# Scaling softmax rows in place on GpSimd, joining the scalars of two head pairs, and reweaving the matmul order of a hybrid attention layer

## The chip, the cores and the metric

The kernel runs on one NeuronCore of a Trainium2 chip. The metric is device microseconds (us) of one execution, from the first to the last instruction of the program. The engines have separate instruction queues: PE (TensorE, matmuls and transposes), DVE (VectorE), ACT (ScalarE), POOL (GpSimd) and SP (SyncE, which here only issues DMAs).

## The reference

One decoder layer on 512 tokens of width 1024, in float32: eight heads of block-sparse attention beside eight heads of a chunked Gated DeltaNet, both from one input projection, then an output projection, an RMS norm, and a squared-ReLU MLP between two further norms. Cut to what the change touches:

```python
h = rms_norm(x, w_first)
q, k, v, gdn_qkv, z, a, b = split(h @ w_in)

# attention: 512 tokens, 8 heads of 64; with a top-3 of 256-wide blocks all blocks are seen
s   = q @ k.T / 8 + rel_bias[distance]       # causal
att = softmax(s) @ v

# DeltaNet: a causal convolution of width 4 and silu on its q, k, v
q, k, v = silu(conv(gdn_qkv));  q, k = l2_normalize(q), l2_normalize(k)
beta, g = sigmoid(b), -exp(a_log) * softplus(a + dt_bias)   # per token and head
# chunks of 64 tokens: T = inverse of (1 + lower triangle of beta * k k^T * decay),
# then 8 chunks one after the other, with the state S (64x64 per head) carried along
o = rms_norm(gdn(q, k, v, beta, g)) * silu(z)

x1  = x + rms_norm(concat(att, o) @ w_out, post_mix)
u   = rms_norm(x1, pre_mlp)
out = x1 + rms_norm(relu(u @ w_up)**2 @ w_down, post_mlp)
```

## The kernel before

**Arithmetic.** Large operands are kept as a sum of two reduced-precision parts, `hi` and `lo`. `split(hi, lo, src)` (L112) copies `src` into `hi` on ACT and writes `lo = src - hi` with one DVE subtraction. A product of two such operands is three matmuls (`mm3`, L144). For weights that come from memory in pieces of 128x512 (`w_raw`), the `lo` part is made on DVE or on POOL; `LO_DVE` (L29) says for which numbers of pieces it is DVE.

**Tiles.** The 512 tokens lie along the columns, so one projection item is one bank of PSUM (128 output columns x 512 tokens, 24 matmuls of 512 columns). `ORDER` (L28) lists the items: `q`, `k`, `v`, `z` are DeltaNet's, `x`, `y` are attention's q and k, `w` is attention's v; the number is the pair of heads, since 128 rows are two heads of 64. `bank(tag)` gives out the eight banks of PSUM: two `mm` (projections), three `g` (DeltaNet), three `a` (attention).

**What sets the order.** PE's order is written out by hand. Every piece of the work is a Python generator (`projections`, `scores`, `values`, `chunks`, `inverse`, `scan`, `output`, ...), and `Weave.run` (L58) takes the next step of one after the other by the text `STEPS` (L20), passing over a generator whose `yield name` waits for a mark that isn't set yet. The matmuls run in exactly that order. The instructions of DVE, ACT, POOL and SP are put in order by a scheduler; `LEAD` gives the steps of a kind of generator a head start in its priorities. So a step that is put elsewhere in `STEPS` takes with it the matmuls, and the work of the other engines follows.

**Places that the change touches:**

- `scores` (L647) computes, for each pair `p`, four score blocks: row block q (128 tokens) against 128, 256, 384 or 512 keys, in the groups (3), (2) and (1, 0). A DVE instruction adds the bias and takes the minimum (`mins`, L675), ACT exponentiates in place in SBUF and adds up the rows (L677). After the last group DVE takes the reciprocals of the sums, ACT spreads them over 64 columns each (`R8`, L683).
- `values` (L688) turns the exponentials with PE transposes (L701; key block k of row blocks k to 3, so 2, 4, 6 and 8 transposes), ACT copies them to SBUF (`ph`, L704). Then four PE transposes turn `R8` (L720), ACT copies the result (L722), the products with V run into the bank `po` (L710), and DVE multiplies by the turned reciprocals (L728) before the split.
- `conv_silu` (L359) scales a projection's bank by the rms factor in place in PSUM, then ACT and three DVE instructions (L365) form the convolution from it. The bank is free after the last of them.
- `chunks` and `turned` (L551, L513), once per pair: ACT gathers the per-token scalars of one pair into `R`, four PE transposes turn it, ACT and DVE make `RC`, matmuls with the selecting matrix `sel` spread its rows (`rows`, L533), and `within` (L539) forms the products inside the 64-token chunks, from which come `NT` and `AT`. After pairs 1 and 3 `NT` goes to memory (`d_n`).
- `inverse` (L735) loads it back in another layout and inverts 32x32 triangles with 62 DVE instructions (`pr`, `inv`, L747 and L748), then stores the result (`d_u`, `d_t`). `scan` (L757) clears `UT` on POOL, loads the two results back, and combines them in two rounds of 32x32 matmuls (`ps_g<-uap,NT`, then `ps_g<-inv,uap`). POOL then makes `kB` and the decayed keys `kdec` for two pairs at a time (L806, L807), on which the matmuls `ps_g<-inv,kB` wait; then come the eight chunk steps.
- `normed` (L990), once per block t of 128 tokens after the output projection: square sums on ACT, the factor by two small POOL instructions (`rstd_of`, L170, with a power), the scaled sum with x on DVE, then the same again for the MLP's norm, and PE transposes.
- `up0` (L1039): the first 512 columns of the MLP's first product, in halves of 256 tokens, so that two blocks of tokens are enough to begin.

Of the kernel before, what the change touches and what calls it, by code (L numbers as in the profile page):

```python
# [21 lines left out]
LEAD = {'chunks': 25, 'inverse': 0, 'scan': 50, 'scores': 400, 'values': 300, 'finish_o': 400, 'take': 50, 'take_a': 300, 'scalars': 0}
TURNS = 0, 2, 1, 3, 4, 6, 5, 7
FILL = 7
SQUARES = {1: (0,), 2: (1,), 3: (2, 3), 4: (4, 5), 5: (6, 7)}
AT_SUM, AT_RSTD = (6, 0), (7, 1)
FIRST_BANKS = "mm g g a"
ORDER = "k0 q0 x0 y0 k1 q2 q1 k2 k3 z0 q3 x1 w0 v3 v0 v1 v2 y1 y2 x2 x3 y3 z2 z3 z1"  # L28
LO_DVE = (23, 51)  # L29
# [1506 lines left out]
```

## Time and profile before

| | |
|---|---|
| median of 3 runs | 612.99 us (612.47 to 614.84) |
| the profiled execution | 613.28 us |
| its span, first to last instruction | 611.5 us |
| granted TensorE clock | 0.999 |
| PE busy | 600.7 us (98%) |
| DVE, ACT, POOL busy | 481.2, 364.8, 140.9 us |
| bytes over DMA | 113.21 MB |

The stages by PE's rows: the head until some 28 us; the projections with the DeltaNet scalars, the scores and the chunk products until 166; the scan's two rounds and its chunk steps until 235, among the last projections; the output projection from 241 to 290; the first MLP group until some 311; the rest of the MLP until 605; then the last norm and the stores. A matmul's busy time includes its pipeline, so that two neighbours overlap: 512 columns show as 0.39 us busy, one beginning every 0.23 us. PE's share of 98% therefore counts overlapped and filled time, and its idle time is what tells.

### The profile page before, as it was taken

Reading aid. Unit: us, or ns where it says so; the run is one execution under the profiler, and the core shown is the slowest. Engines: PE = TensorE matmul, PEld = TensorE weight load, DVE = VectorE, ACT = ScalarE, POOL = GpSimd, SP = SyncE. Lnnn points to the kernel's source line nnn. Section 1 sums busy time; section 2 is a strip of 40 time slices with the busy share of each in tenths; the row PEclk is TensorE's granted clock in tenths of the full one; section 3 lists DMA queues with packets and bytes.
Section 4 is the critical chain, followed back from the end, with each engine's and each line's share of the span. In section 5 each row is a group of like instructions: output and inputs, shape, how many; then the busy total and the mean of one; then the engine's idle time right before and its main releaser. Section 6 shows DMA issues by size and latency. Waiting matters only on the chain.

```text
span 611.5 us, 11058 instructions
## 1 busy us (share of the span) xinstructions
PE 600.7 (98%) x4281; PEld 515.0 (84%) x4281; DVE 481.2 (79%) x692; ACT 364.8 (60%) x645; POOL 140.9 (23%) x180
## 2 busy tenths in 40 slices
PE   9999999999999999999999999999999999999995
PEld 7778788877778786888999999999998888888884
DVE  6688975999664866668799888787798888887776
ACT  7379772353677567444368565755575657565663
POOL 1557745001221111025022231122221310000000
PEclk9999999999999999999999999999999999999999
DMA  9332334227412124815879899998999999767503
GB/s 316 89 115 86 88 87 117 91 70 184 125 45 66 35 89 128 286 53 173 329 176 311 219 274 223 273 283 205 235 337 357 285 293 286 254 229 297 164 0 138
DMA packets 61156, 113.21 MB, mean 185 GB/s; under 512 B 15784, under 2 KB 35368, under 8 KB 60720
## 3 DMA queue, kind: packets, MB, share of 16 engines
q1 hardware_dynamic: 43120, 82.89, 40.0%
q0 software_dynamic: 17696, 29.36, 23.2%
q8 instruction: 33, 0.54, 0.4%
q10 hardware_dynamic: 288, 0.26, 0.1%
q14 instruction: 19, 0.16, 0.1%
HBM read 106.71 MB, written 35.15 MB: 232 GB/s over the span
## 4 chain that ended last, share of the span: by engine, by line
PE 58%; issue 9%; DMA 2%; ACT 2%; DVE 0%; POOLq 0%; SPq 0%
PE ps_mm L82 27%; PE ps_g L82 17%; PE ps_a L82 13%; DMA xy<-d_x 1%; DMA wo_raw<-in_w_out 1%; PE ps_a L85 1%; ACT wo_h L125 0%; ACT ph L704 0%; ACT L L677 0%; DVE wo_l L126 0%; DVE wdl L114 0%; ACT wdh L113 0%; PE ps_g L85 0%; POOLq L1532 0%; ACT ot L876 0%
## 5 line engine op out<-in xcount | busy, mean ns | idle before, releaser
L113 ACT CAST wdh<-wd 128x1024 fp32r<-128x1024 f32 x53 | 55.9, 1054 | 51.4 <-PE ps_mm L82 22.6
L113 ACT CAST u_h<-w 128x1024 fp32r<-128x1024 f32 x49 | 50.9, 1044 | 52.1 <-DVE w L1146 15.6
L114 DVE TENSOR_TENSOR wdl<-wd,wdh 128x1024 fp32r<-128x1024 f32 x53 | 64.9, 1224 | 21.6 <-ACT wdh L113 21.4
L114 DVE TENSOR_TENSOR u_l<-w,u_h 128x1024 fp32r<-128x1024 f32 x49 | 59.8, 1224 | 23.8 <-ACT u_h L113 23.8
L82 PE MATMUL ps_mm<-hT_h,w_hi 128*128 128x512 f32 x168 | 71.3, 424 | 1.3 <-DVE conv L365 1.0
L82 PE MATMUL ps_mm<-hT_h,w_lo 128*128 128x512 f32 x168 | 66.1, 394 | 0.0
L1179 POOL DMA_DIRECT2D d_T<-in_w_down x32 | 33.0, 1032 | 142.3 <-DMA d_T<-in_w_down 81.3
L82 PE MATMUL ps_mm<-hT_l,w_hi 128*128 128x512 f32 x168 | 65.7, 391 | 0.0
L137 ACT CAST w_hi<-w_raw 128x512 fp32r<-128x512 f32 x50 | 31.0, 620 | 46.1 <-DMA w_raw<-in_w_in 12.0
L82 PE MATMUL ps_mm<-wdh,u_h 128*128 128x512 f32 x116 | 45.3, 390 | 0.0
L82 PE MATMUL ps_mm<-wdl,u_h 128*128 128x512 f32 x116 | 45.1, 389 | 0.0
L82 PE MATMUL ps_mm<-wdh,u_l 128*128 128x512 f32 x116 | 45.1, 389 | 0.0
L82 PEld LDWEIGHTS ps_mm<-hT_h,w_hi 128*128 128x128 f32 x168 | 31.7, 189 | 12.4 <-issue 5.9
L82 PEld LDWEIGHTS ps_mm<-hT_h,w_lo 128*128 128x128 f32 x168 | 31.5, 188 | 7.5 <-DVE w_lo L138 0.4
L82 PEld LDWEIGHTS ps_mm<-hT_l,w_hi 128*128 128x128 f32 x168 | 31.8, 189 | 4.9
L138 POOL TENSOR_TENSOR w_lo<-w_raw,w_hi 128x512 fp32r<-128x512 f32 x23 | 29.7, 1291 | 20.3 <-ACT w_hi L137 17.4
L114 DVE TENSOR_TENSOR u_l<-f,u_h 128x1024 fp32r<-128x1024 f32 x28 | 34.1, 1218 | 0.0
L82 PE MATMUL ps_g<-wdh,u_h 128*128 128x512 f32 x80 | 31.1, 389 | 0.0
L82 PE MATMUL ps_g<-wdl,u_h 128*128 128x512 f32 x80 | 31.1, 389 | 0.0
L82 PE MATMUL ps_g<-wdh,u_l 128*128 128x512 f32 x80 | 31.1, 389 | 0.0
L113 ACT CAST u_h<-f 128x1024 fp32r<-128x1024 f32 x28 | 29.3, 1046 | 0.0
L138 DVE TENSOR_TENSOR w_lo<-w_raw,w_hi 128x512 fp32r<-128x512 f32 x27 | 21.4, 794 | 7.9 <-ACT w_hi L137 7.8
(486 smaller groups left out, 1830.2 us busy)
## 6 DMA issues: line engine op xcount, KB each, us to landing
d_T<-in_w_down POOLq DMA_DIRECT2D x48, 512.0 KB, 11.0
wd<-d_T SPq DMA_DIRECT2D x32, 512.0 KB, 6.2
w<-in_w_up SPq DMA_DIRECT2D x28, 512.0 KB, 7.6
wd<-in_w_down SPq DMA_DIRECT2D x24, 512.0 KB, 7.3
w_raw<-in_w_in SPq DMA_DIRECT2D x40, 256.0 KB, 2.6
wo_raw<-in_w_out SPq DMA_DIRECT2D x16, 256.0 KB, 3.5
d_T<-d_T POOLq DMA_DIRECT2D x8, 512.0 KB, 12.1
ww<-in_w_first SPq DMA_DIRECT2D x8, 256.0 KB, 5.3
```

Of the source, the lines that this page charges most:

```text
L82: nc.tensor.matmul(o, l, r, **kw)
L85: nc.tensor.transpose(o, i, ident[:k, :k])
L113: nc.scalar.copy(hi, src)
L114: tt(lo, src, f32(hi), op=OP.subtract)
L137: nc.scalar.copy(hi, raw)
L138: (sub or tt)(lo, raw, f32(hi), op=OP.subtract)
L1179: nc.gpsimd.dma_start(d_T[t][k], block(b, second)[k], accum_op=OP.add, max_dma_last_dim=1024)
```

## The change

- **Softmax.** `scores` takes the reciprocals of the row sums per group, and POOL multiplies the rows of exponentials in place (`tensor_scalar`, 32 instructions: for each of 8 heads 512, 384, 256 and 128 columns). The marks that let `values` begin come after that. The spreading copy, the four transposes, their copy and the DVE multiplication per pair are gone; `split` reads the product from PSUM.
- **Scalars of two pairs.** `turned(z)` fills `R` for two pairs and turns it with four transposes, `RC` has 64 rows for two pairs, `sel` has nine planes in place of five (one DMA and one copy more). `matrices(z)` forms the chunk products of both pairs in one step; the stores of `NT` stand behind the second.
- **Norm.** In `normed` the bank is multiplied by the weight before the factor is known; the factor is made by ACT's square root and DVE's reciprocal, and enters with the sum. POOL has no part in it.
- **Convolutions.** Those of v (four) and of q of pair 3 write the scaled projection to SBUF and read it from there.
- **up0.** The last of the four 128-column pieces is done 512 tokens wide at the end, the third is in two steps.
- **Order.** `STEPS`, `LEAD`, `ORDER` and `LO_DVE` are new: POOL makes `w_lo` of pieces 0 to 18 and from 67 on (before 0 to 22 and from 51 on). Some buffers of the output weights take another tag.

```diff
-ORDER = "k0 q0 x0 y0 k1 q2 q1 k2 k3 z0 q3 x1 w0 v3 v0 v1 v2 y1 y2 x2 x3 y3 z2 z3 z1"
-LO_DVE = (23, 51)
+ORDER = "k0 q0 x0 y0 k1 q1 q2 k3 k2 x1 z0 q3 w0 v0 v1 v3 y1 v2 x2 y2 y3 x3 z1 z3 z2"
+LO_DVE = (19, 67)
...
-    def conv_silu(p, ft, dst, apart=False):
-        tt(p, p, rb, op=OP.mult)
+    def conv_silu(ps, ft, p, dst, apart=False):
+        tt(p, ps, rb, op=OP.mult)
...
-            conv_silu(ps, p, q, p % 2)
+            sq = tmp("sqt")
+            conv_silu(ps, p, sq if p == 3 else ps, q, p % 2)
...
-            conv_silu(ps, 8 + p, v)
+            conv_silu(ps, 8 + p, v, v)
...
-    RC = [RCs[p % 2] for p in range(4)]
+    RC = [RCs[p // 2] for p in range(4)]
...
+    def matrices(z):
+        ps = (2 * z, 2 * z + 1)
+        for p in ps:
+            yield f"E{p}"
+            yield f"q{p}"
         yield
-        yield f"q{p}"
-        O = within(p)
-        for hh in range(2):
-            tt(NT[:, 2 * p + hh], O[hh][:, :, 0], AT[:, 2 * p + hh], op=OP.mult)
...
+        Os = {p: within(p) for p in ps}
+        b3 = {}
+        for p in ps:
+            b3[p] = rows(p, 1)
+            for hh in range(2):
+                tt(NT[:, 2 * p + hh], Os[p][hh][:, :, 0], AT[:, 2 * p + hh], op=OP.mult)
...
-                yield
+                both = slice(min(group), max(group) + 1)
+                nc.vector.reciprocal(sums[:, both], sums[:, both])
+                for q in group:
+                    for hh in range(2):
+                        l = rows_of[p, hh, q]
+                        nc.gpsimd.tensor_scalar(l, l, sums[:, q, hh:hh + 1], None, op0=OP.mult)
                 for q in group:
                     mark(f"row{p}{q}")
-            nc.vector.reciprocal(sums, sums)
-            sums_of[p] = at.tile([128, 512], FT, name="R8", bufs=1)
-            nc.scalar.copy(sums_of[p].rearrange("p (q h e) -> p q h e", q=4, h=2), sums[:, :, :, None].to_broadcast([128, 4, 2, 64]))
-            mark(f"sums{p}")
+                yield
...
-            yield f"sums{p}"
-            rs = bank("a")
-            for q in range(4):
-                transpose(rs[:, 128 * q:128 * q + 128], sums_of[p][:, 128 * q:128 * q + 128])
-            sums_of[p] = at.tile([128, 512], FT, name="t2")
-            nc.scalar.copy(sums_of[p], rs)
+            yield
             yield
             po = bank("a")
             for k in (3, 2, 1, 0):
                 product(k, P[k])
-            mx = at.tile([128, 512], FT, name="t2")
-            tt(mx, po, sums_of[p], op=OP.mult)
-            split(mx_h[0][:, p], mx_l[0][:, p], mx)
+            split(mx_h[0][:, p], mx_l[0][:, p], po)
...
         for b in range(2):
-            act(sq[:, 512 * b:512 * b + 512], P[b], AF.Square, accum_out=ss[:, b:b + 1])
-        tt(s1, ss[:, 0:1], ss[:, 1:2], op=OP.add)
-        r = rstd_of(s1, s1, 1024)
-        for b in range(2):
             bs = slice(512 * b, 512 * b + 512)
-            stt(sq[:, bs], P[b], r, nb[:, 0, bs], op0=OP.mult, op1=OP.mult)
-        tt(x1, x1, sq, op=OP.add)
+            act(sq[:, bs], P[b], AF.Square, scale=1 / 32, accum_out=ss[:, b:b + 1])
+            if b == 0:
+                nc.vector.tensor_scalar(ss[:, 0:1], ss[:, 0:1], EPS, None, op0=OP.add)
+            tt(sq[:, bs], P[b], nb[:, 0, bs], op=OP.mult)
+        act(s1, ss[:, 1:2], AF.Sqrt, bias=ss[:, 0:1])
+        nc.vector.reciprocal(s1, s1)
+        stt(x1, sq, s1, x1, op0=OP.mult, op1=OP.add)
...
-        for j in range(4):
-            part(j, 0, 256)
-            yield
+        for j in range(3):
+            for ks in ((range(8),) if j < 2 else (range(4), range(4, 8))):
+                part(j, 0, 256, ks)
+                yield
         yield "n3"
         for j in range(4):
-            part(j, 256, 512)
+            part(j, 256 if j < 3 else 0, 512)
...
-STEPS = "chunks1 constants_in0*2 chunks3 bias0*2 scalars0 scores0 ..."
-LEAD = {'chunks': 25, 'inverse': 0, 'scan': 50, 'scores': 400, 'values': 300, 'finish_o': 400, 'take': 50, 'take_a': 300, 'scalars': 0}
+STEPS = "bias0 constants_in0 inverse0 bias0 constants_in0 scalars0 ev_q0 ..."
+LEAD = {'chunks': 300, 'inverse': 25, 'scan': 100, 'scores': 400, 'values': 100, 'finish_o': 400, 'take': 100, 'take_a': 0, 'scalars': 200}
```

Over the whole program PE has 3710 instructions in place of 3758, DVE 708 for 694, ACT 593 for 597, POOL 193 for 185, SP 240 for 239. Three places show how the order has moved. The rows are those of one engine's queue in its order, with the source line, the operation, the output and its inputs, and the size; `x6` stands for six alike in a row.

**DVE, just ahead of the inverse.** `NT` and `AT` are the chunk products, `LWQ` holds the scaled keys and queries, and `pr` begins the inverse. Before:

```order
L365 SCALAR_TENSOR_TENSOR conv<-ps_mm,cw,conv 128x509
L579 TENSOR_TENSOR NT<-ps_g,AT 128x256
L579 TENSOR_TENSOR NT<-ps_a,AT 128x256
L587 TENSOR_TENSOR LWQ_99<-LWQ_99,ps_g 128x4x128
L370 SCALAR_TENSOR_TENSOR LWQ_99<-th,conv 128x4x64 x2
...
L579 TENSOR_TENSOR NT<-ps_g,AT 128x256
L579 TENSOR_TENSOR NT<-ps_a,AT 128x256
L587 TENSOR_TENSOR LWQ_99<-LWQ_99,ps_g 128x4x2x64
L586 TENSOR_TENSOR AT<-ps_g,AT 128x256
L586 TENSOR_TENSOR AT<-ps_a,AT 128x256
L747 TENSOR_TENSOR pr<-inv 128x31
```

And now:

```order
L363 SCALAR_TENSOR_TENSOR conv<-sqt,cw,conv 128x509
L566 TENSOR_TENSOR LWQ_101<-kraw,ps_g 128x4x2x64
L368 SCALAR_TENSOR_TENSOR LWQ_101<-th,conv 128x4x64 x2
L566 TENSOR_TENSOR LWQ_101<-kraw,ps_g 128x4x128
L586 TENSOR_TENSOR NT<-ps_g,AT 128x256
L586 TENSOR_TENSOR NT<-ps_a,AT 128x256
L595 TENSOR_TENSOR AT<-ps_g,AT 128x256
L595 TENSOR_TENSOR AT<-ps_a,AT 128x256
L586 TENSOR_TENSOR NT<-ps_g,AT 128x256
L586 TENSOR_TENSOR NT<-ps_a,AT 128x256
L596 TENSOR_TENSOR LWQ_101<-LWQ_101,ps_g 128x4x128
...
L751 TENSOR_TENSOR pr<-inv 128x31
```

Both pairs' chunk products now stand together, behind the convolution of q3, whose input is an SBUF tile.

**POOL, around the scan's start.** `L` are the rows of exponentials, `S` the scan's state, `inv` the cleared `UT`. Before:

```order
L138 TENSOR_TENSOR w_lo<-w_raw,w_hi 128x512 x5
L759 MEMSET inv 128x2048
L824 MEMSET S_2329 128x512
L824 MEMSET S_2330 128x512
L806 TENSOR_TENSOR kB<-kdec,kbe 128x512 x2
L807 TENSOR_TENSOR kdec<-kdec,egd 128x4x128 x2
L806 TENSOR_TENSOR kB<-kdec,kbe 128x512 x2
L807 TENSOR_TENSOR kdec<-kdec,egd 128x4x128 x2
```

And now:

```order
L763 MEMSET inv 128x2048
L810 TENSOR_TENSOR kB<-kdec,kbe 128x512 x2
L692 TENSOR_SCALAR L<-L,sums 128x384 x2
L811 TENSOR_TENSOR kdec<-kdec,egd 128x4x128 x2
L692 TENSOR_SCALAR L<-L,sums 128x256 x2
L692 TENSOR_SCALAR L<-L,sums 128x128 x2
L810 TENSOR_TENSOR kB<-kdec,kbe 128x512 x2
L811 TENSOR_TENSOR kdec<-kdec,egd 128x4x128 x2
L692 TENSOR_SCALAR L<-L,sums 128x512 x2
L692 TENSOR_SCALAR L<-L,sums 128x384 x2
```

The rows of pair 1 stand among the first `kB` and `kdec`, and the 512-column rows of pair 2 behind the second `kB` and `kdec`.

**PE, the scan's two rounds and the values of pair 1.** `uap` and `inv` are the loaded halves of the inverse, `pt` the attention's q and k, `hT` and `w` a projection. Before:

```order
L85 MATMUL ps_a<-ident,L 128x128 x6
L82 MATMUL ps_g<-uap,NT 32x32 x64
L85 MATMUL ps_a<-ident,L 128x128 x8
L85 MATMUL ps_a<-ident,R_1946 128x128 x4
L82 MATMUL ps_g<-inv,uap 32x32 x64
L82 MATMUL ps_a<-pt 128x512 x6
```

And now:

```order
L82 MATMUL ps_g<-uap,NT 32x32 x64
L82 MATMUL ps_mm<-hT_h_85,w_hi 128x512
L82 MATMUL ps_mm<-hT_l_87,w_hi 128x512
L82 MATMUL ps_mm<-hT_h_85,w_lo 128x512
L85 MATMUL ps_a<-ident,L 128x128 x6
...
L85 MATMUL ps_a<-ident,L 128x128 x8
...
L82 MATMUL ps_a<-pt 128x512 x6
L82 MATMUL ps_g<-inv,uap 32x32 x64
```

The four transposes of `R8` are gone, and three groups of projection matmuls, the transposes of the exponentials and the next scores now stand between the rounds.

More of the change, by code (lines that the diff above doesn't have):

```diff
@@ L510, in layer, with turned @@
     RCs = [gpool.tile([128, 512], FR, name=f"RC{p}") for p in range(2)]
[L511 to L519 removed]
+    RC = [RCs[p // 2] for p in range(4)]
+    def turned(z):
+        yield "scalars"
+        for p in (2 * z, 2 * z + 1):
+            yield f"k{p}"
+        if z:
+            yield "R0"
+        zs = slice(4 * z, 4 * z + 4)
+        rk = rq[0]
+        nc.gpsimd.tensor_tensor(rkb[:, :, zs], rk[:, :, zs], beta[:, :, zs], op=OP.mult)
+        nc.gpsimd.tensor_tensor(rrb[:, :, zs], rkb[:, :, zs], rk[:, :, zs], op=OP.mult)
+        mark(f"rkb{z}")
+        for p in (2 * z, 2 * z + 1):
+            hs, Rp = slice(2 * p, 2 * p + 2), R[:, :, 32 * (p % 2):32 * (p % 2) + 32]
+            for i in range(2):
+                nc.scalar.copy(Rp[:, :, 8 * i:8 * i + 8].rearrange("p t (n h) -> p t n h", h=2), by4[:, :, :, hs].rearrange("p n t h -> p t n h"))
+            for c in range(2):
+                a, b = slice(64 * c, 64 * c + 64), slice(64 - 64 * c, 128 - 64 * c)
+                nc.scalar.copy(Rp[a, :, 16:32].rearrange("p t (s i) -> p t s i", s=2)[:, :, :, 4:6], gc[b, :, None, hs].to_broadcast([64, 4, 2, 2]))
         yield
         p_R = transposed(lambda t: R[:, t])
[L522 to L528 removed]
+        mark(f"R{z}")
+        RH = tmp("RH", FR)[:64]
+        RT = tmp("RT")[:64]
+        nc.scalar.copy(RH, p_R[:64])
+        act(RT, f32(RH), AF.Identity, scale=su[:64, 0:1])
+        stt(RCs[z][:64], p_R[:64], su[:64, 1:2], RT, op0=OP.mult, op1=OP.add)
+        mark(f"RC{z}")
     RG = gpool.tile([128, 4, 8], FR, name="RG")
@@ L534, in rows @@
         o = bank()
-        mm(o, sel[:, i], RC[p], start=True, stop=True)
+        mm(o, sel[:, 5 * (p % 2) + i], RC[p], start=True, stop=True)
         return o
@@ L551, in chunks @@
     def chunks(p):
-        yield "scalars"
-        yield f"k{p}"
-        if p:
-            yield f"R{p - 1}"
-        if p > 1:
-            yield f"RC{p - 2}"
-        hp = slice(2 * p, 2 * p + 2)
-        rk = rq[0]
-        nc.gpsimd.tensor_tensor(rkb[:, :, hp], rk[:, :, hp], beta[:, :, hp], op=OP.mult)
-        nc.gpsimd.tensor_tensor(rrb[:, :, hp], rkb[:, :, hp], rk[:, :, hp], op=OP.mult)
-        mark(f"rkb{p}")
-        yield from turned(p)
-        nc.scalar.copy(RG[32 * p:32 * p + 32, p], f32(RC[p][:32, 0:512:64]))
+        yield f"RC{p // 2}"
+        yield
+        own = slice(32 * (p % 2), 32 * (p % 2) + 32)
+        nc.scalar.copy(RG[32 * p:32 * p + 32, p], f32(RC[p][own, 0:512:64]))
         b1 = rows(p, 0)
@@ L568, in chunks @@
         for hh in range(2):
-            mm(ep[:, hh], sel[:, 2 + hh], c8(RC[p])[:, :, 0], start=hh == 0, stop=hh == 1, skip_group_check=True)
-        b3 = rows(p, 1)
-        mark(f"RC{p}")
+            mm(ep[:, hh], sel[:, 5 * (p % 2) + 2 + hh], c8(RC[p])[:, :, 0], start=hh == 0, stop=hh == 1, skip_group_check=True)
         for hh in range(2):
@@ L924, in weights_out @@
                 for k in range(4):
-                    tag, bufs = ("w_raw", 2) if b == 0 or (z, k) < (1, 2) and z else ("w_hi", 3) if (z, k) > (1, 0) or k < 1 else ("w_lo", 3)
+                    n = len(W)
+                    tag, bufs = (("w_raw", 2) if n % 4 < 2 else ("t2", 2)) if b == 0 else ("w_raw", 2) if z and k < 2 else ("w_hi", 3) if z or k < 1 else ("w_lo", 3)
                     load_split(wh[:, k], wl[:, k], w_out[512 * z + 128 * k:512 * z + 128 * k + 128, 512 * b:512 * b + 512],
-                               raw=wpool.tile([128, 512], FT, name="wo_raw", tag=tag, bufs=bufs))
+                               raw=(at if tag == "t2" else wpool).tile([128, 512], FT, name="wo_raw", tag=tag, bufs=bufs))
                     W[b, 4 * z + k] = (wh[:, k], wl[:, k])
@@ L1066, in layer @@
     nc.gpsimd.memset(R, 0.0)
+    for z in range(2):
+        spawn(turned(z), LEAD["chunks"])
+        spawn(matrices(z), LEAD["chunks"])
     for p in range(4):
@@ L1072, in layer @@
     spawn(main)
-    weave.run({"inverse", "chunks3", "v0", "v1", "v2", "v3"})
+    weave.run({"inverse", "chunks1", "v0", "v1", "v2", "v3"})
     sP.close()
```

69 lines of the change are left out of this document (30 added, 39 removed).

## The prediction

> **What bounds the kernel now.** I read the page's busy times first, then a table by stages, then PE's list of waits and its own rows at those places.
>
> ```profile
> PE 600.7 (98%) x4281; PEld 515.0 (84%) x4281; DVE 481.2 (79%) x692; ACT 364.8 (60%) x645; POOL 140.9 (23%) x180
> ```
>
> PE is the bound; POOL is nearly free. The stages (span, then PE, PEld, DVE, ACT, POOL busy with instruction counts, clock, DMA share, GB/s):
>
> ```profile
> 100.00:140.00 40.00, 40.00 (x195) 31.63 (x194) 36.19 (x85) 16.37 (x30) 4.26 (x4) 1.00 0.29 99
> 140.00:150.00 10.00, 9.02 (x44) 7.18 (x43) 9.50 (x17) 3.68 (x6) 1.81 (x1) 1.00 0.70 207
> 150.00:160.00 10.00, 9.65 (x48) 7.07 (x46) 7.53 (x14) 2.96 (x6) 5.54 (x6) 1.00 0.81 138
> 160.00:170.00 10.00, 10.00 (x191) 7.95 (x189) 6.22 (x22) 9.40 (x29) 0.00 (x0) 1.00 0.42 128
> 170.00:180.00 10.00, 9.73 (x218) 6.47 (x221) 7.06 (x18) 6.35 (x16) 4.07 (x4) 1.00 0.03 7
> 180.00:230.00 50.00, 50.00 (x695) 40.03 (x687) 32.55 (x76) 33.31 (x86) 7.47 (x12) 1.00 0.21 65
> 230.00:240.00 10.00, 8.51 (x56) 6.03 (x55) 6.37 (x13) 9.02 (x24) 2.79 (x4) 1.00 0.35 107
> 240.00:311.00 71.00, 71.00 (x422) 62.83 (x420) 52.45 (x64) 28.72 (x56) 14.99 (x21) 1.00 0.58 204
> 311.00:600.00 289.00, 289.00 (x1829) 263.23 (x1828) 241.47 (x233) 182.26 (x221) 44.17 (x54) 1.00 0.89 246
> ```
>
> PE has no idle time outside four windows: 0.98 + 0.35 + 0.27 + 1.49 = 3.1 us. From 240 to 600 it never waits, so the MLP starts earlier by what the stages ahead give back, and nothing else in it changes. What it waited for:
>
> ```profile
> PE ps_a L85 <- ACT L L677: 1.4, 2, 0.8
> PE ps_mm L82 <- DVE conv L365: 1.0, 1, 1.0
> PE ps_a L82 <- DVE mins L675: 0.3, 1, 0.3
> ```
>
> ```profile
> 144.28 0.47 PE L82 MATMUL ps_mm<-hT_h,w_hi 128*128 128x512 f32 x1 [0.98 <-DVE conv L365]
> 230.79 0.55 PE L85 MATMUL ps_a<-ident,L 128*128 128x128 f32 x3 [0.63 <-ACT L L677]
> 232.15 0.55 PE L85 MATMUL ps_a<-ident,L 128*128 128x128 f32 x3 [0.81 <-ACT L L677]
> ```
>
> So a gain has two possible sources: matmuls removed, and these waits.
>
> **Matmuls removed.** The chain of waits gives PE's cadence when nothing holds it:
>
> ```profile
> 245.96 4.76 PE ps_g L82 x21
> 289.39 0.87 PE ps_a L85 x8
> 290.27 2.87 PE ps_mm L82 x24
> ```
>
> 512 columns take 4.76/21 = 0.227 us, a transpose 0.87/8 = 0.109, 256 columns (up0, the third row) 2.87/24 = 0.120. Four pairs lose four transposes of `R8` each (16), two joint gathers in place of four lose 8: 24 × 0.109 = 2.61 us. In up0 the piece done 512 wide has 24 matmuls for 48: 24 × (2 × 0.1196 − 0.2267) = 0.30. Together **−2.9 us**, which needs only that PE stays the bound.
>
> **Waits removed.** The wait at 144.28 is a projection's bank held by a convolution of v until its third DVE instruction; now the bank is free after the first multiplication. I take all 0.98. The two waits at 230.79 and 232.15 are for the last pair's exponentials; the new order puts five projection groups of three matmuls ahead of those transposes after the last scores' turn, 15 × 0.227 = 3.4 us, more than the 1.44 waited. The 0.27 at 170 lay between the scan's two rounds, which followed each other behind transposes alone; now 4.3 us of other matmuls stand between (nine projections 2.0, fourteen transposes 1.5, scores 0.7). For the 0.35 at 150 I see the scores' groups further apart too. **−3.1 us** in all; start-to-start gaps at these places, counted instead of idle time, make it 4.4, which I keep for the range.
>
> **The new waits.** Four things could take their place.
>
> *(a) The inverse.* Its input is both pairs' `NT`:
>
> ```profile
> 93.82 0.41 DVE L579 TENSOR_TENSOR NT<-ps_a,AT 128x256 f32<-128x256 f32 x1
> 102.42 0.21 DVE L747 TENSOR_TENSOR pr<-inv 128x31 f32<-128x31 f32 x1 [6.92 <-DMA inv<-d_n]
> 140.46 1.10 DVE L751 COPY inv<-inv 128x1024 f32<-128x1024 f32 x1
> 142.79 0.68 DVE L138 TENSOR_TENSOR w_lo<-w_raw,w_hi 128x512 fp32r<-128x512 f32 x1
> 166.98 1.31 PE L82 MATMUL ps_g<-uap,NT 32*32 32x32 f32 x128
> ```
>
> The round trip through memory took 102.42 − 94.2 = 8.2 us. In the changed queue the chunk products of pairs 2 and 3 stand together and behind the convolution of q3; counted on PE's order by the cadences above they come some 5.7 us later. So the inverse starts at about 108.1. It took 39.1 us, with 24 other instructions among its 63. By the new order about 17 more stand there (w_lo of pieces that POOL made before, convolutions, splits): 17 × 0.68 = 11.5. Against that, POOL's own w_lo blocked some of it:
>
> ```profile
> 103.96 2.56 POOL L138 TENSOR_TENSOR w_lo<-w_raw,w_hi 128x512 fp32r<-128x512 f32 x2 [3.55 <-ACT w_hi L137]
> 104.00 1.38 DVE L747 TENSOR_TENSOR pr<-inv 128x112 f32<-128x112 f32 x1
> 105.41 1.24 DVE L748 TENSOR_TENSOR inv<-inv,pr 128x112 f32<-128x112 f32 x1
> 106.69 0.30 DVE L747 TENSOR_TENSOR pr<-inv 128x135 f32<-128x135 f32 x1
> ```
>
> The 112-column steps took 1.38 and 1.24 while POOL ran, the larger 135-column one 0.30; with a third such step 3.0 us, which go, since POOL's last w_lo then come before the inverse. End: 108.1 + 39.1 + 11.5 − 3.0 = 155.7, where it was 141.6. Behind it stand the stores and the loads:
>
> ```profile
> 145.39 1.81 POOL L759 MEMSET inv<- 128x2048 f32 x1 [35.45 <-DMA d_t<-inv]
> 150.85 1.49 SPq L764 DMA_DIRECT2D uap<-d_t  x3
> ```
>
> The stores landed 3.9 us after the copy (145.39 − 141.56); the loads need some 2 us of issue and, by my estimate from the same round trip, 2 more: `uap` at 163.6. Round 1 began at 166.98 without waiting; in the new order it has about 0.8 us more PE work ahead of it and some 1.3 us of idle time less, so it is wanted at 166.5. Cover 2 to 3 us: cost 0. With DVE this full, a bank of x2 is given back late by my count of its queue, 0 to 1.6 us; I take 0.8.
>
> *(b) POOL in front of the scan.* The rows' price isn't in the trace: there is no large one-input multiplication on POOL. The bounds are
>
> ```profile
> L609 POOL CAST L<-L 128x640 fp32r<-128x640 f32 x1 | 0.7, 724 | 0.0
> L138 POOL TENSOR_TENSOR w_lo<-w_raw,w_hi 128x512 fp32r<-128x512 f32 x23 | 29.7, 1291 | 20.3 <-ACT w_hi L137 17.4
> 171.50 2.06 POOL L806 TENSOR_TENSOR kB<-kdec,kbe 128x512 f32<-128x512 f32 x2 [14.19 <-PE ps_g L82]
> 173.51 2.06 POOL L807 TENSOR_TENSOR kdec<-kdec,egd 128x512 f32<-128x512 f32 x2
> ```
>
> a one-input copy, 0.724/640 × 512 = 0.58 us for 512 columns, and a two-input instruction, 1.03 to 1.29. A row scaled by one number per partition reads one tensor, so I take the copy's price and a little: 0.62. A pair has 2 × 1280 columns, five times 512: 3.1 us and 0.06 for each of eight instructions, some 3.6; 14 us in all, beside PE. At the other end it is 5.2 to 6.5 a pair. One place is tight: pair 2's 512-column rows now stand behind the second `kB` and `kdec`, and `values` of that pair behind them. By its order and the cadences PE has 6.0 us of other matmuls, POOL's line is 5.5 to 6.4 at the low price, 6.9 to 7.8 at the high one: 0 to 1.9, I take 0.3.
>
> *(c) The last pair's rows.* From the last scores to the transposes that need them PE has 7.3 us of other work; minimum, exponential, reciprocal, two small scalings take 5.5 to 6.5: 0 to 1, I take 0.3. *(d) Norm.* Block 3 before, and the table load of the last norm, which moves here:
>
> ```profile
> 286.13 0.39 PE L82 MATMUL ps_g<-wo_h,ma_l 128*128 128x512 f32 x1
> 293.80 1.28 DVE L1007 SCALAR_TENSOR_TENSOR xs<-xs,s,nb 128x1024 f32<-128x1024 f32 x1 [0.98 <-POOL s L175]
> ...
> 597.18 1.28 ACT L1395 ACT_TABLE_LOAD   x1
> ```
>
> From the last product, 286.5, to 295.1 the chain was 8.6 us. Without POOL's four small steps and with the two weightings ahead of the factor I count 5.8, that load of 1.28 us included; PE's order has 8.1 us of other matmuls behind it (block 0: 8.2 against 8.9). Cost 0; were the cover gone, the difference up to 8.6 − 5.8 would show.
>
> The removed copies on ACT and the DVE multiplication cost nothing off PE's path; PE hides them up to the margins named.
>
> **Sum.** Against the profiled execution's 613.28: −2.9 − 3.1 + 0.8 + 0.3 + 0.3 = 608.7; that execution stood 0.3 above the median, so **608.4 to 608.6**; I say 608.6. Anything under 0.5% (3.1 us) is about what a measurement of this kernel can't tell from no change.
>
> [...]
>
> **The rivals.** *Old waits return* (chance 0.2): the reweaving only trades one wait for another of the same size, since other parts of the order are as tight. Then −2.9 alone: 613.28 − 2.9 − 0.3 = 610.1. For it: the margins in (b) and (c) are under a microsecond. Against it: the conv wait has a cause that is gone. This is also the case that half of the change doesn't do what it says.
>
> *POOL's scaling is slow and blocks DVE* (0.16): 1.29 per 512 columns. Then (b) costs 1.9 in place of 0.3, (c) 1.0 for 0.3, and some two blocked DVE steps of 1.1 us each, by the row at 104.00, delay a bank: 608.6 + 1.6 + 0.7 + 2.2 = 613.
>
> *The inverse is late* (0.12), the side on which it is slower: DVE carries the inverse with 41 others, and each step needs the one before. The cover is 2 us; each further microsecond stands on PE, since the matmuls between are in a fixed order and cannot fill in. It decides from a loss of about 2 us on DVE; 616.5 needs 10 us, which is nine steps blocked by 1.1 us, or 15 more instructions of 0.68 than I counted. DVE was 36.19 of 40 us busy in 100 to 140, which speaks for it; POOL's nearly empty 4.26 there speaks against blocking.
>
> **The numbers.** My forecast 0.52, the others 0.20, 0.16 and 0.12. The forecast lies 1.3 us under the 0.5% bound of 609.9, so nearly all of its chance is "faster", with a little from the first rival: 0.53. Same: 0.35, from both middle rivals. Slower than 616.1: 0.12. The low end is all waits gone by start-to-start gaps and no new one, 613.28 − 2.9 − 4.4 − 0.3 = 605.7. The high end, 614.0, takes in slow scaling and one further microsecond; the late inverse is left out. The likeliest case alone has 606.5 to 609.9.
>
> **What would show it.** Right: 24 transposes fewer, no wait on `conv`, the inverse ending at 154 to 157 with round 1 not waiting on `uap`, POOL's 512-column scaling at 0.6 to 0.7 us. Wrong: PE waiting on POOL's `L` or `kB`; round 1 waiting on a DMA; a scaling row above 1 us; DVE steps of the inverse above 1 us; a wait for the norm's transposes behind the table load.

## The result, and the profile after

The changed kernel takes 616.81 us (median, 615.66 to 618.44) where the kernel before took 612.73 on the same chip: a ratio of 1.0068, interval 1.0051 to 1.0085. It is slower by 0.7%; 608.6 had been forecast. The profiled execution took 617.81, span 616.0. Two executions of the experiments below, one each of e8 and e16, ran at a clock of 0.753 and took 738 us; the times and ratios given are those of the others.

The busy times, and the list of what PE waited for from 20 to 311 us (us in total, times, longest):

```profile
PE 600.5 (97%) x4233; PEld 512.8 (83%) x4233; DVE 479.0 (78%) x706; ACT 361.4 (59%) x641; POOL 164.8 (27%) x188
```

```profile
PE ps_mm L82 <- ACT mg_h L112: 1.9, 1, 1.9
PE ps_a L85 <- POOL L L692: 1.4, 3, 0.7
PE ps_mm L82 <- POOL w_lo L135: 1.2, 2, 1.0
PE ps_g L82 <- ACT vn L858: 1.1, 2, 0.6
PE ps_mm L82 <- DVE conv L363: 0.8, 1, 0.8
PE ps_a L85 <- POOL rstd L228: 0.4, 1, 0.4
PE ps_mm L82 <- DVE pt L635: 0.3, 1, 0.3
PE ps_a L82 <- ACT AT L572: 0.3, 1, 0.3
PE ps_a L85 <- POOL oss L174: 0.2, 1, 0.2
```

The names: `mg_h` is the high part of DeltaNet's gated output, `vn` the copy that ACT makes in each chunk step of the scan, `rstd` the factor of the first norm, `oss` the factors of DeltaNet's norm, `pt` the high and low parts of attention's q and k, `L` the rows of exponentials, and `AT` the decays that go into the chunk products.

PE stays the bound and waits on nine things for 7.6 us in place of three entries for 2.7. The old waits are gone: the convolution wait in this list is another, at 46 us, in a pair whose convolution still works in PSUM. The table by stages, cut finer where something changed:

```profile
140.00:150.00 10.00, 10.00 (x49) 8.29 (x49) 9.96 (x24) 3.50 (x6) 0.00 (x0) 1.00 0.26 82
150.00:160.00 10.00, 10.00 (x49) 7.62 (x50) 9.35 (x24) 4.54 (x9) 2.85 (x2) 1.00 0.38 127
160.00:170.00 10.00, 9.34 (x55) 6.88 (x55) 7.84 (x24) 5.75 (x18) 9.56 (x9) 1.00 0.85 200
170.00:180.00 10.00, 9.56 (x303) 7.02 (x303) 5.24 (x13) 6.25 (x15) 6.58 (x9) 1.00 0.36 99
180.00:190.00 10.00, 9.31 (x186) 6.81 (x183) 5.49 (x20) 9.35 (x31) 9.65 (x10) 1.00 0.28 82
240.00:245.00 5.00, 2.98 (x10) 1.20 (x10) 3.90 (x7) 3.77 (x8) 0.00 (x0) 1.00 0.98 309
245.00:250.00 5.00, 5.00 (x16) 3.96 (x15) 4.28 (x8) 2.23 (x4) 0.00 (x0) 0.66 1.02 396
311.00:600.00 289.00, 289.00 (x1828) 263.27 (x1827) 241.36 (x230) 180.26 (x216) 45.14 (x56) 1.00 0.90 248
```

Three things are new: POOL is full where the scan begins (9.56 and 9.65 of 10 us), PE loses 2 of 5 us at 240, and the granted clock is 0.66 in the 5 us after that. Measured from one matmul's start to the next, beyond the usual cadence, the new losses are:

| place | caused by | us |
|---|---|---|
| 27, 65, 69, 169–174, 185, 237 | POOL: `rstd` 0.6, `w_lo` 1.5, `L` 2.2, `oss` 0.4 | 4.7 |
| 244 | output projection's first input `mg_h` late 2.35; then 1.4 of slow matmuls | 3.75 |
| 46, 84–102, 166, 217, 230 | `conv` 0.95, `AT` 0.95, `pt` 0.5, `vn` 1.7 | 4.1 |

Together 12.5. Of POOL's 4.7, the rows of exponentials account for 3.7 (`L` and `w_lo`). `rstd` runs on POOL before the first row is scaled (at 49.6), and POOL began `oss` 0.08 us after its input had come from DVE. The old waits, 4.4 in this measure, are gone, and 2.9 of matmuls: 613.28 − 2.9 − 4.4 + 12.5 = 618.5, beside 617.81 profiled.

**POOL's rows.** The groups of the scaling by shape (busy us, mean ns of one):

```profile
L692 POOL TENSOR_SCALAR L<-L,sums 128x512 f32<-128x512 f32 x8 | 13.8, 1726 | 45.9 <-DVE inv L752 44.9 <-DVE sums L688 1.0
L692 POOL TENSOR_SCALAR L<-L,sums 128x384 f32<-128x384 f32 x8 | 10.4, 1310 | 2.3 <-DVE sums L688 2.3
L692 POOL TENSOR_SCALAR L<-L,sums 128x256 f32<-128x256 f32 x8 | 7.7, 978 | 7.1 <-DVE sums L688 7.0
L692 POOL TENSOR_SCALAR L<-L,sums 128x128 f32<-128x128 f32 x8 | 5.1, 652 | 0.0
```

512 columns take 1.73 us in the mean, not 0.62 (six of the eight took 1.56 to 1.60; the other two, 1.85 and 2.54, raise the mean); all 32 rows take 37 us, not 14. What stands behind them in POOL's queue (its timeline), and PE's row that waits for the last:

```profile
59.09 2.99 POOL L692 TENSOR_SCALAR L<-L,sums 128x256 f32<-128x256 f32 x4
62.05 2.09 POOL L174 TENSOR_TENSOR rk<-rk,mhalf 128x8 f32<-128x8 f32 x1
64.11 1.26 POOL L135 TENSOR_TENSOR w_lo<-w_raw,w_hi 128x512 fp32r<-128x512 f32 x1
182.03 5.61 POOL L692 TENSOR_SCALAR L<-L,sums 128x512 f32<-128x512 f32 x4
```

```profile
65.42 0.50 PE L82 MATMUL ps_mm<-hT_h,w_lo 128*128 128x512 f32 x1 [0.96 <-POOL w_lo L135]
185.19 0.33 PE L85 MATMUL ps_a<-ident,L 128*128 128x128 f32 x1 [0.69 <-POOL L L692]
```

At 65 PE waits not for a row but for a piece of weights queued behind four of them and a small step.

**The output projection's start.** A DVE instruction, SP's loads, a second DVE instruction and ACT's queue, in time order; then PE, and what SP's queue waited for from 215 to 240:

```profile
228.17 0.69 DVE L434 SCALAR_TENSOR_TENSOR zs<-t,zs 128x512 f32<-128x512 f32 x1
228.88 10.16 SPq L121 DMA_DIRECT2D wo_raw<-in_w_out  x13
239.58 0.75 DVE L907 SCALAR_TENSOR_TENSOR om<-ps_g,nw,zs 128x512 f32<-128x512 f32 x1
242.07 1.25 ACT L122 CAST wo_h<-wo_raw 128x512 fp32r<-128x512 f32 x2 [0.20 <-DMA wo_raw<-in_w_out]
243.23 0.61 ACT L112 CAST mg_h<-om 128x512 fp32r<-128x512 f32 x1
```

```profile
243.90 0.50 PE L82 MATMUL ps_mm<-wo_h,mg_h 128*128 128x512 f32 x1 [1.95 <-ACT mg_h L112]
```

```profile
SPq L121 <- DVE zs L434: 6.4, 1, 6.4
```

The change puts every second pair of the first output weights' buffers under the tag `t2`, which the gate (`zs`, the silu of z) uses too. SP's queue stands still for 6.4 us until the gate's last read of `t2`, at 228.86; then 13 loads go out in the 10.2 us that follow. The casts of what they bring stand in ACT's queue ahead of `mg_h`, whose input was ready at 240.33 and which starts 2.9 us later. From 245.8 on seven matmuls come 0.43 us apart in place of 0.227, at the reduced clock.

**The inverse.** Start and final copy, in DVE's timeline:

```profile
111.39 0.38 DVE L751 TENSOR_TENSOR pr<-inv 128x31 f32<-128x31 f32 x1 [3.83 <-DMA inv<-d_n]
157.16 1.17 DVE L755 COPY inv<-inv 128x1024 f32<-128x1024 f32 x1
```

### The profile page after: what moved, and what is told of

Read it like the earlier page. It is cut to its first block, busy times and chain, and to the rows that moved or that the text cites. A ratio compares the mean times of both kernels' runs of the same rounds, so it can differ in the third digit from the quotient of the medians.

```text
span 616.0 us, 11001 instructions
## 1 busy us (share of the span) xinstructions
PE 600.5 (97%) x4233; PEld 512.8 (83%) x4233; DVE 479.0 (78%) x706; ACT 361.4 (59%) x641; POOL 164.8 (27%) x188
## 4 chain that ended last, share of the span: by engine, by line
PE 56%; issue 10%; POOL 2%; DMA 2%; DVE 1%; ACT 1%; POOLq 0%; SPq 0%
PE ps_mm L82 27%; PE ps_g L82 17%; PE ps_a L82 12%; PE ps_a L85 1%; POOL L L692 1%; DMA xy<-d_x 1%; DMA wo_raw<-in_w_out 1%; POOL kdec L811 1%; DVE wo_l L123 0%; PE ps_g L85 0%; ACT vn L858 0%; ACT L L686 0%; ACT wo_h L122 0%; DVE wdl L113 0%; POOL kB L810 0%
## 5 line engine op out<-in xcount | busy, mean ns | idle before, releaser
L692 POOL TENSOR_SCALAR L<-L,sums 128x512 f32<-128x512 f32 (+3 forms) x32 | 36.9, 1166 | 55.4 <-DVE inv L752 44.9
L135 POOL TENSOR_TENSOR w_lo<-w_raw,w_hi 128x512 fp32r<-128x512 f32 x19 | 25.5, 1340 | 20.1 <-ACT w_hi L134 16.9
```

Of the source, the lines that this page charges most:

```text
L135: (sub or tt)(lo, raw, f32(hi), op=OP.subtract)
L692: nc.gpsimd.tensor_scalar(l, l, sums[:, q, hh:hh + 1], None, op0=OP.mult)
```

## The experiments

In those that start from the changed kernel PE's order is the same (e12 differs in two rows, e16 by the 16 that it adds), and e6 has PE's order of the kernel before. The queues of DVE, ACT and POOL are laid out anew by due times, so a one-line edit also moves other work a little. Ratios are to the kernel before on the same chip; the changed kernel stands at 1.0068. A ratio is good to some 0.0015 either way, so a difference of two of them to about 1.3 us.

### Which part costs: scaling and buffers

```diff
# e1: the four lines go              # e3: on VectorE
-                        nc.gpsimd.tensor_scalar(l, l, sums[:, q, hh:hh + 1], None, op0=OP.mult)
+                        nc.vector.tensor_scalar(l, l, sums[:, q, hh:hh + 1], None, op0=OP.mult)
# e2: tags of the output weights as before;  e4: e2 and e3 together
-                    tag, bufs = (("w_raw", 2) if n % 4 < 2 else ("t2", 2)) if b == 0 else ...
+                    tag, bufs = ("w_raw", 2) if b == 0 or z and k < 2 else ...
```

> The changed kernel without the 32 multiplications of the softmax rows on POOL (the rows stay unnormalized; reciprocals, marks and order are kept). The changed kernel takes 616.8 us. Theory P: POOL needs 37.1 us for these rows (1.73 us for 512 columns) and hands it on to PE: waits for L 2.2 us from start to start, for POOL's w_lo 1.5, for the small factors before o 0.4. Then 612.7 us, and no wait on POOL L or POOL w_lo is left. Rival O: the order is tight everywhere, and what is taken away here comes back at the next late thing: 615.5 to 616.8. The wait for mg_h at the output projection (2.1 us) stays by both.

613.89 us, 1.0014 [0.9998, 1.0029]: 3.3 us less than the changed kernel (0.0054 × 612.7). All waits on POOL's `L` and `w_lo` are gone, and the gain is about what they cost. It isn't theirs alone: the wait for `mg_h`, which was to stay, fell from 1.9 to 0.6 with no slow matmuls behind it, and a new wait stands in PE's list, at 239.6.

```profile
PE ps_a L82 <- ACT ph L715: 1.8, 1, 1.8
```

> The changed kernel with the output weights' raw pieces in the buffers of before (w_raw for all of the first half, none in t2). Theory B: the fourth load waited until 228.88 for the t2 buffer that z3's gate held, the loads crowded together behind it, ACT stood before their casts, and the cast of mg_h behind them came 2.9 us late; PE waited 2.1 us, and seven matmuls afterwards ran at 0.43 us in place of 0.227, 1.4 us more, under a lower granted clock. Without it 613.1 us, a granted clock of 0.998 to 0.999, and the wait for mg_h under 0.5 us. Rival M: the loads are held by memory bandwidth (the DMA engines were 98 to 102% busy from 240 to 250), so that the buffers change nothing: 616.3 to 617.

615.02, 1.0033 [1.0018, 1.0048]: 2.1 us less, where theory B had 3.7. The `mg_h` wait and the low clock behind it are gone from the profiled execution (e1 and e3, with the changed tags, show no low clock there either: the mean is 0.998 in e2 and e3, 0.999 in e1), and a copy 12 us earlier is late instead (e4 shows what stands ahead of it):

```profile
PE ps_g L82 <- ACT vn L858: 1.8, 2, 1.3
```

> The changed kernel with the 32 multiplications on DVE in place of POOL. Theory P: the waits on POOL go as without scaling, and DVE, which isn't PE's bound outside the inverse, takes some 0.3 to 0.7 us for 512 columns, 7 to 14 us in all: 613 to 614 us. Rival O: 616 or more, as DVE's other work (banks given back, w_lo) comes late instead.

615.76, 1.0038 [1.0022, 1.0054]: 1.8 us less, close to rival O and not theory P's 613 to 614. A row costs VectorE less than a third of what it costs POOL (0.535 us beside 1.73 for 512 columns), but a bank of x2 comes back later for it:

```profile
L692 DVE TENSOR_SCALAR L<-L,sums 128x512 f32<-128x512 f32 x8 | 4.0, 535 | 0.0
PE ps_mm L82 <- DVE pt L635: 1.6, 1, 1.6
```

> Both: the multiplications on DVE, and the output weights in the buffers of before. If theories P and B hold and their parts add up, 609.5 to 610.5 us, under the 612.7 of the kernel before. If they share a wait (POOL's small factors lie on the way to mg_h), 611 to 613.

613.24, 0.9997 [0.9981, 1.0013]: 4.4 us less, where the two parts alone sum to 3.9. The causes add up within the error, each smaller than its theory had it, and the kernel ties with the one before instead of beating it. What is left, PE first, then ACT's row that stands ahead of the copy:

```profile
228.93 0.68 PE L82 MATMUL ps_g<-vn,AT 64*64 64x64 f32 x16 [2.08 <-ACT vn L858]
225.22 0.62 ACT L122 CAST wo_h<-wo_raw 128x512 fp32r<-128x512 f32 x1 [2.62 <-DMA wo_raw<-in_w_out]
```

ACT stands 2.6 us before a cast whose weights haven't landed, and `vn`, which PE wants, is queued behind it.

### With both causes out

e18 is e1 with e2's tags: no scaling anywhere, old buffers.

> No scaling of the rows at all (the output isn't normalized), old buffers. Additive: 613.9 - 2.1 = 611.8. Prediction's sum if POOL's price and the buffers were its only errors: 608.6. If the order's own waits stay: 611.5 to 613.

612.81, 0.9995 [0.9980, 1.0010]. With no POOL row and no shared tag it only equals the kernel before. PE's list:

```profile
PE ps_g L82 <- ACT vn L858: 2.6, 2, 2.1
PE ps_a L85 <- ACT ph L715: 1.8, 1, 1.8
PE ps_a L82 <- ACT AT L572: 1.2, 2, 1.0
PE ps_mm L82 <- DVE conv L363: 0.8, 1, 0.8
PE ps_mm L82 <- DVE pt L635: 0.3, 1, 0.3
```

6.7 us stand here in five waits that the kernel before hadn't (two more of 0.2 us are left out), and in this execution 3.4 us of half clock follow the one on `ph`:

```profile
237.71:241.12 3.41, 3.41 (x16) 1.36 (x14) 2.54 (x5) 2.01 (x4) 0.00 (x0) 0.50 0.47 130
```

So the 6 us forecast as gain are taken back by waits that belong to neither cause alone. No run separates what makes them: the matmul order, the joined scalars, the order of ACT's queue. The tags have a part, since `vn` costs 2.6 us with the old ones and 1.3 in e1 with the new. The two causes come on top, with 4.5 us between this kernel and the changed one (0.0073 × 612.7), less than the 4.7 and 3.75 of the table above, since `ph` and `vn` grow where they go.

### The removed matmuls

e16 is e4 with four transposes of `ident` per pair put back.

```diff
+            rs = bank("a")
+            for q in range(4):
+                transpose(rs[:, 128 * q:128 * q + 128], ident)
```

> Rows on DVE and old buffers, with four transposes of the identity put back per pair where those of R8 stood. The prediction's first term: 16 x 0.109 = 1.74 us, so 614.9 to 615.2 from 613.2. If they only fill time in which PE would wait for ph or kB, 613.2 to 613.8.

615.31, 1.0034 [1.0017, 1.0051], 2.3 us over e4 (1.74 by the cadence; its profiled span is 2.0 longer). The term is real; its size is shown only to within the 1.3 us. DVE's and ACT's queues shifted a little too. The other eight transposes and the 0.30 of up0 have no run of their own; PE's 4281 instructions fell to 4233, as counted.

### Parts put into the order before

```diff
# e6: before, with the convolutions of v and of q3 reading SBUF
-            conv_silu(ps, 8 + p, v)
+            conv_silu(ps, 8 + p, v, v)
# e7: before, with POOL's rows (R8, its transposes and copies gone)
+                        nc.gpsimd.tensor_scalar(l, l, sums[:, q, hh:hh + 1], None, op0=OP.mult)
# e8: before, with rows on VectorE, e6, the late norm factor, up0's wide piece
+        act(s1, ss[:, 1:2], AF.Sqrt, bias=ss[:, 0:1])
+        nc.vector.reciprocal(s1, s1)
+        stt(x1, sq, s1, x1, op0=OP.mult, op1=OP.add)
```

> The kernel before (612.9 us) with only the convolutions of v and q3 read from SBUF, in the order of before. My prediction gave this part 0.98 us for the wait at 144.28: 611.8 to 612.0, no wait on conv left. Rival: the bank freed early only moves PE to the next wait behind the same busy DVE (102 to 141 carried the inverse): 612.6 to 613.2.

615.19, 1.0033 [1.0018, 1.0047]: 2 us slower, not 1 faster. The wait on `conv` is gone, as designed; two others came:

```profile
PE ps_g L82 <- DVE RC L527: 1.5, 1, 1.5
PE ps_g L85 <- DVE vt L370: 1.3, 1, 1.3
```

Ahead of `RC` in DVE's queue a small instruction ran beside POOL's `w_lo`, for 1.24 us where it took 0.18 before:

```profile
87.34 1.24 DVE L591 TENSOR_TENSOR kbe<-by 128x32 f32<-128x32 f32 x1
```

One convolution row from SBUF took 1.02 us there (0.75 elsewhere), and `RC` now stands behind another instruction. It began at 92.48 in place of 89.93.

> The kernel before with only the softmax rows scaled on POOL (no R8, no turning of it: 16 transposes fewer, 1.7 us of PE), in the order of before. Theory P: POOL needs some 37 us for them, so PE waits for L and for w_lo: 613 to 616 in spite of 1.7 us less work. Rival W: the price on POOL is harmless where the order was not rewoven around it: 611 to 611.5.

639.87, 1.0439 [1.0416, 1.0462], far beyond both expectations. In the old order PE waits on the rows and on the scalars queued behind them in POOL (`R`); its mean granted clock fell to 0.981:

```profile
PE ps_a L85 <- POOL L L683: 9.1, 7, 3.5
PE ps_g L85 <- ACT R L516: 8.1, 2, 4.9
```

> The kernel before, in its own order, with four parts of the change: rows scaled on DVE (13 us there by the run with DVE scaling), convolutions in SBUF, late norm factor, the wide piece in up0. PE's work falls by 1.7 + 0.3 us. If the order of before carries them: 609.9 to 611. If DVE, which the inverse fills from 102 to 141, passes its new work on to PE: 612.5 to 614.

621.26, 1.0158 [1.0132, 1.0183]: 3.4 us of waits on the rows, now on DVE, e6's two, and shorter ones. In the order of before these parts don't pay.

e12 is the reverse: the changed kernel with those convolutions in PSUM again.

> The changed kernel with the convolutions of v and q3 read from PSUM again. My prediction's step: the bank is held longer and PE waits again for conv, one or more times about 1 us: 617.5 to 619. Rival, by the run of that part alone in the kernel before, which was 1.8 us slower and waited for the convolution's result instead: the part brings nothing, 616 to 617.

624.39, 1.0198 [1.0171, 1.0224], 8 us over the changed kernel. Banks come back late three times; the wait at 46 stood in the changed kernel too, those of 3.8 and 0.6 us are new, and 3.4 us of half clock follow the longest.

```profile
PE ps_mm L82 <- DVE conv L363: 5.2, 3, 3.8
```

The same edit loses 2 us in one order and saves some 8 in the other.

### A cheaper scaling, other buffers

e9 scales on POOL by a two-input instruction with a broadcast factor, e10 is that with the old tags, e11 has the old tags, pair 1 like e9 and the others on VectorE, e17 one head of each pair like e9 and the other on VectorE:

```diff
+nc.gpsimd.tensor_tensor(l, l, sums[:, q, hh:hh + 1].to_broadcast(list(l.shape)), op=OP.mult)
```

> The changed kernel with the rows still scaled on POOL, but by a two-input multiplication with the reciprocals broadcast along the row, the form of kB, which took 1.03 us for 512 columns where the scaling by one number per partition took 1.73. Theory P, the price decides: POOL needs 20 to 24 us for the rows in place of 37, so about half of what leaving them out gave (3.7 us of span): 614.8 to 615.5 from 616.8, POOL waits for L under 1 us in all. Rival S: what hurts is that the rows stand in POOL's queue ahead of w_lo, kB and the small factors, whatever they cost: 616.3 to 617. If the two-input form costs 1.3 us or more, no difference.

616.32, 1.0049 [1.0032, 1.0067]: 1.2 us less, which the error doesn't tell from none. The instruction that reads two operands is the faster one on POOL (1.26 us beside 1.73 for 512 columns), but at 26 us for all rows not as cheap as theory P had it:

```profile
L692 POOL TENSOR_TENSOR L<-L,sums 128x512 f32<-128x512 f32 x8 | 9.9, 1263 | 45.8 <-DVE inv L752 44.9 <-DVE sums L688 0.9
```

The waits on `L` are gone, but `rstd` grew to 1.1, `AT` to 1.2 and `conv` to 1.3.

> The same with the old buffers for the output weights, whose part measured 2.1 us alone. Theories P and B together: 612.7 to 613.5. If the two share a wait, 614 to 615.

614.28, 1.0020 [1.0009, 1.0032], the second of the two forecasts.

> Old buffers, rows of pairs 0, 2 and 3 on DVE, those of pair 1, which stand where DVE still ends the inverse, on POOL in the two-input form. With all rows on DVE PE waited 1.7 us for a bank (pt at 165.9) behind them. If that is DVE's load there, the wait falls to 0.5 and the time from 613.2 to 612; if the rows of pair 1 are late from POOL instead, 613 to 613.6.

613.07, 1.0003 [0.9989, 1.0018], a tie: the late bank of x2 costs 0.8 in place of 1.7, `rstd` 1.35 more.

> Old buffers; of each pair one head's rows on DVE (6.5 us in all), the other's on POOL in the two-input form (13 us). If the load on one engine was what made the rows late, both rows come in half the time: no wait for L, the wait for pt at 166 under 0.9: 611.5 to 612.5. If the order's own waits (conv at 46, AT at 100, vn at 229, some 4 us in the traces) rule, 612.8 to 613.5.

616.72, 1.0061 [1.0036, 1.0085]: halving the load didn't help. Run side by side, VectorE's row takes 1.02 us in the mean where it took 0.535 in e3:

```profile
L695 DVE TENSOR_SCALAR L<-L,sums 128x512 f32<-128x512 f32 x4 | 4.1, 1024 | 0.0
L693 POOL TENSOR_TENSOR L<-L,sums 128x512 f32<-128x512 f32 x4 | 4.9, 1228 | 45.9 <-DVE inv L755 45.0 <-DVE sums L688 0.7 <-PE ps_mm L82 0.2
```

Seven of e3's eight took 0.48 us; here three of four took 0.98 to 1.37, and beside the one at 0.48 POOL's took 1.30 where 1.04 was its shortest. What makes them longer side by side no run shows.

The last four try to free ACT from the late casts of e4: e5 makes the first eight on POOL; e13 gives every third weight a buffer of its own; e14 is e11 with that buffer and with piece 8's `w_lo`, which stood ahead of `rstd` in POOL's queue, on VectorE; e15 is e13 with that `w_lo` moved.

```diff
# e5
+                               cast=nc.scalar.copy if b else nc.gpsimd.tensor_copy)
# e13, e14, e15
+                    own = b == 0 and len(W) % 3 == 2
+                    tag, bufs = ("own", 1) if own else ("w_raw", 2) if b == 0 or z and k < 2 else ...
# e14, e15
+        load = lambda n: ended(begin(n), None if n == 8 or LO_DVE[0] <= n < LO_DVE[1] else nc.gpsimd.tensor_tensor)
```

> The kernel with the rows scaled on DVE and the old buffers, and the hi casts of the first eight output-weight pieces on POOL in place of ACT. Theory A: what is left of the loss ahead of the output (2.25 us on vn at 228.9, 0.75 on ph at 237) is ACT standing before casts whose piece has not landed, with the copies for PE queued behind them. Then both waits go, and the time falls from 613.2 to 610.3 to 611. Rival: the copies are late by themselves (scan's chain PE to ACT to PE), or POOL's factors for o come late behind the casts: 612.5 to 613.5.

615.10, 1.0025 [1.0007, 1.0042], slower than e4. The casts now stand ahead of POOL's small factors for `o`: a wait on `ot` of 1.9 us is new, and `vn` still takes 1.6.

> Rows on DVE, output weights' raw pieces in the old two buffers and one of their own (the space of R8 is free). Theory A: the loads go through two buffers, each bound by its own round trip, ACT waits for them with the copies of vn queued behind; a third buffer brings them earlier: the wait on vn at 229 falls from 2.2 us to under 1, the time from 613.2 to 611.5. Rival: the scheduler puts the casts earlier as well, and ACT waits as before: 613 to 613.6.

616.14, 1.0049 [1.0031, 1.0068]. ACT's queue is laid out anew and stands before casts again: `vn` 3.0, `ph` 2.4 in PE's list. The remedy failed.

> The same, with pair 1's rows on POOL in the two-input form, and the w_lo that stood before rstd in POOL's queue on DVE. If the wait for rstd (1.35 us there) comes from that w_lo, it falls under 0.3, and with the third buffer the time goes from 613.1 to 610 to 611, under the kernel before. If DVE hands the moved w_lo on at the head, 612 to 613.

615.39, 1.0039 [1.0025, 1.0053]. The `rstd` wait is gone, as expected of the moved `w_lo`; `vn` stays, at 3.0 in PE's list.

> As e13, with the w_lo ahead of rstd on DVE. With rows on DVE alone the wait for rstd was under 0.3 us in the traces, so this should bring at most 0.3 over e13: 611 to 611.5; if the w_lo on DVE delays the first banks given back, 612 to 613.

616.26, 1.0056 [1.0030, 1.0083]. The same again: no wait on `rstd`, 2.8 on `vn`. No version beats the kernel before; e1, e4, e11 and e18 tie with it, and e1 and e18 leave the scaling out.

## Why the prediction was wrong, and where it was right

- **Matmuls removed, −2.9:** right as far as it was tried. e16 puts 16 of them back for 2.3 us, where 1.74 was their share.
- **Waits removed, −3.1:** the named waits went, but as a gain the term failed. It counted a freed wait as time won without asking what is late next. e6 frees the convolution wait alone and loses 2 us, with waits on `RC` and `vt` in its place; e18 has all three gone and 6.7 us of others. This is what the first rival ("old waits return") described, with a larger size than its 3.
- **New waits, +1.4:** the term that was most mis-sized; about 12.5 by start-to-start gaps, of which 4.7 through POOL, 3.75 at the output's start, 4.1 at other places.
- **The price of POOL's rows in (b):** the step that failed was the choice "a row scaled by one number per partition reads one tensor, so I take the copy's price". It measured 1.73 us (1.56 at its shortest), above even the bound taken from the two-input rows, 1.29. At the tight place, pair 2's rows at 185, PE lost 0.9 where 0.3 was taken. VectorE took 0.535 us for the same row (e3). The second rival had slow rows, the right place and too low a price (613). Of the DVE blocking that it named little shows: beside POOL's first rows of pair 1, at 158 to 161, two DVE instructions took 1.11 and 1.03 us where 0.68 is usual, no step of the inverse before its last copy took over 1 us, and the convolution rows from SBUF took 0.75 us, as from PSUM.
- **Who stands behind them:** (b) looked at `kB`, `kdec` and `values` only. A place that cost as much lay elsewhere in POOL's queue: `w_lo` at 65 and 69 us, 1.5 in all. `rstd` at 27, 0.6, stands behind a `w_lo` and ahead of all rows; it stays in e1, and e14 and e15, which move that `w_lo`, have no wait on it. Taking the rows off POOL is worth 1.8 us if VectorE does them (e3), 3.3 if nobody does (e1).
- **"From 240 to 600 it never waits … nothing else in it changes":** failed at 244. The tags of the output weights were in the description of the change, and no term priced them; e2 shows 2.1 us.
- **(a) the inverse:** right in mechanism and nearly in size. It started at 111.4 (108.1 forecast; 109.6 in e4, without POOL's stalls ahead of it), took 46.9 us (47.6) and ended at 158.3 (155.7), and the first round at 170.27 didn't wait. The slower-side rival did not happen; the slowdown had other causes. The late bank of x2 cost 0.5 (0.8 taken).
- **(c):** no wait on the last pair's rows; at 230 PE waits 0.63 for `vn`, which wasn't on the list. **(d)** norm and up0: no wait from 250 to 600, cost 0 as forecast.

What stays open: which part of the change makes the waits that are left in e18, and whether an ordering of ACT's casts exists that frees `vn` and `ph`. Every placement tried moved the wait or left it.

## What to carry to other kernels

When a tight order is rewoven, price the gain of a removed wait only up to the next late item, and look for that item in the queues of the *other* engines: what stands behind a slow instruction (here `w_lo` behind 2.99 us of rows) or behind a cast whose load hasn't landed (`vn` in e4, behind 2.62 us of waiting). An edit of buffer tags is an edit of the load order (SP's queue stood 6.4 us for `t2`): list who holds the tag last. And a new form of instruction has no price until a row with that form shows it; the price of a neighbour, with fewer operands or with more, was no bound here (0.58 and 1.03 to 1.29 us for 512 columns, where the new form took 1.73).

## What the runs showed of the hardware

- On POOL a multiplication of 128x512 f32 by a per-partition scalar took 1.73 us in the mean, the same by a broadcast tensor 1.26 (e9), VectorE's `tensor_scalar` 0.535 (e3). At the low end, where five or more of each eight lie, it is some 1.57, 1.05 and 0.48 us. One in POOL's timeline:

```profile
159.68 1.57 POOL L692 TENSOR_SCALAR L<-L,sums 128x512 f32<-128x512 f32 x1
```

- In the changed kernel's profile the granted clock fell after a PE wait of 1.95 us that ended at 243.90. It was at half for 3.41 us:

```profile
245.60:249.01 3.41, 3.41 (x10) 2.66 (x9) 3.37 (x6) 1.24 (x2) 0.00 (x0) 0.50 1.02 407
```

The same length of half clock follows the wait of 1.8 us at 236.6 in e18. After one of 2.08 us at 228.93 in e4 the clock stayed at 1.00 (from 230 to 250). What decides it no run shows. The drop doesn't come at this length in every execution: 3.41 us at half take 0.0028 off the mean clock of 616 us, and three of the eight executions had a mean of 0.998.
